# Two heads of the HGRN2 layer in one strand: the level products of both kept together on TensorE

## The chip, the cores and the metric

The kernel runs on one core of a Trainium2 chip. The metric is the device time of one launch in microseconds (us). The core's engines are TensorE (PE in the profile, PEld its weight loads), VectorE (DVE), ScalarE (ACT), GpSimd (POOL) and SyncE (SP); each works through its own queue in order, and they meet through semaphores.

## The reference

Two layers on x of shape 1 x 512 x 1024, float32. Layer 0 (mLSTM heads and sparse attention) is the same in both kernels. Layer 1 is cut here to what matters:

```python
h = rms_norm(x, norm_w[1])
fp, iv, qp, z = jnp.split(h @ w_in + b_in, 4, axis=-1)
logf = jnp.log(lb + (1.0 - lb) * jax.nn.sigmoid(fp))
k = (1.0 - lb) * jax.nn.sigmoid(-fp)
q = jax.nn.silu(qp)
# per head (8 heads of 128 channels):
#   S_t = diag(f_t) S_{t-1} + k_t v_t^T ;  o_t = S_t^T q_t
o = hgrn2_chunkwise(heads(q), heads(k), heads(iv), heads(logf))
o = rms_norm(o, head_norm)
x = x + (o * jax.nn.silu(z)) @ w_out
```

## The kernel before, in words

**Products.** A float32 product is made of three products of rounded operands: high by high, high by low, low by high. ACT writes the high half of a weight block (`whi`), VectorE the low half (`wlo`), 128 x 1024 at a time. One such product is a matmul of 128x512, the "large product" below; its results go to the banks `mx` and `my`.

**Layer 1.** The projection is cut into groups: `t0` to `t3` (forget and query columns of two heads each), `p0` and `p1` (a Strassen-like pair for the value and gate columns, whose extra operands are `ss`), then the output projection `o10`, `o11`. The list is in L2130 to L2140, in the order t0, p0, t1, t2, t3, p1, o10, o11. `t_evac` (L2071 to L2097) empties a `t` group: for each head it makes `f` and the tile `HB`, 128 x 3 x 512, which holds q, q times f, and k. `ivgg` is the tile of values and gates, filled by VectorE and multiplied on POOL.

**A head.** After the second head of a group, `t_evac` starts a strand `hgrn(h)` (L1888 to L2010) for each of the two. It computes the decayed scores of q and k by seven levels, l = 0 to 6, in which positions are joined into blocks of 2, 4, ... 128. Each level has small float32 products on TensorE, into a bank `sd` for levels 0 to 4 and `tq` for 5 and 6: 16 of 32x64 for level 0, 16 of 32x16 for levels 1 to 4, 8 of 32x32 for level 5, 4 of 64x64 for level 6. Then VectorE multiplies half of `HB` by products of the forget gates (`HB<-HB,f` at level 0, `HB<-HB,tt` after it), and the next level's products wait for that. After level 4 `copy_predicated` brings the scores into `AL`, and ACT copies them into the tile `f`. The state work follows: transposes (`tq<-cs,HB`), ACT's copy `kT`, products `tq<-ivgg,kT`, three VectorE steps into `Sx`, the output products `tq<-ivgg,f` and `tq<-Sx,HB`, squares on ACT, a root on POOL, four scaled copies `yo` on VectorE, four transposes `tq<-cs,yo`, and the copies `y1h` (ACT) and `y1l` (VectorE), which the output projection reads.

**What sets the order.** Nothing is issued as it is written. `Flow` (L452 to L516) runs the strands by rank; a strand yields what it waits for: marks, and free slots (`SDS` for an `sd` bank, `TQS` for a `tq` bank). `nlv` lets at most two heads be in their levels. The operations are recorded by `Plan` (L166 to L414), which schedules them over the engines with modelled costs, in several rounds, keeps the best, and then issues them all from one line, L410; so every instruction of the profile has that line, and tiles tell them apart. An operation recorded with `_join` must follow the one recorded before it on TensorE with nothing between: `Plan.edges` (L251 to L259) chains them and gives all their conditions to the first.

```python
        for a, b in zip(self.ops, self.ops[1:]):
            if a.eng == "T" == b.eng and (b.join or len(a.cols) < 4 and a.load == b.load and a.cols[0] < b.cols[0]):
                a.next = b
```

Layer 1 begins at about 340 us of the trace and runs to its end.

Of the kernel before, what the change touches and what calls it, by code (L numbers as in the profile page):

```python
# [15 lines left out]
I32 = mybir.dt.int32  # L16
AF = mybir.ActivationFunctionType
OP = mybir.AluOpType
# [10 lines left out]
HBN = 4  # L29
# [589 lines left out]
def build(tc, I, out):  # L619
# [6 lines left out]
    with ExitStack() as ctx:  # L626
# [24 lines left out]
        def sd_t():  # L651
            return pt("sd", 2)

        def tq_t():
            return pt("tq", 2)
# [324 lines left out]
        with ExitStack() as c0:  # L980
# [3 lines left out]
            def s_t(name, shape, bufs=2, dt=F32):  # L984
                return sp.tile(shape, dt, name=name, tag=name, bufs=bufs)
# [841 lines left out]
        with ExitStack() as c1:  # L1827
# [57 lines left out]
                    fl.mark(E1(n))  # L1885
                u_end(2)

            def hgrn(h):  # L1888
                yield [None, lambda: nlv[0] < 2, SDS]
                nlv[0] += 1  # L1890
                HB, f = HBs[h], fs[h]
                lv = sd_t()
                al, AT = AL[h % 2], cut(f, (4, 128))
                tot, toff, to = f, 0, 0
                tt = s_t("tt", [128, 512], 2)
                te = s_t("te", [128, 4], HBN)
                for l in range(7):
                    L = 1 << l
                    if l < 5:
                        for t in range(4):  # L1900
                            for b in range(4):
                                o = 128 * t + 32 * b
                                if l == 0:
                                    T.matmul(lv[32 * b:32 * b + 32, 64 * t:64 * t + 64], HB[:, 2, o:o + 32],
                                             cust(HB, [[512, 2], [1, 32]], o), start=True, stop=True,
                                             skip_group_check=True)
                                else:
                                    oo = 256 + 64 * (l - 1) + 16 * t
                                    T.matmul(lv[32 * b:32 * b + 32, oo:oo + 16], HB[:, 2, o:o + 32],
                                             cust(HB, [[2 * L, 16 // L], [1, L]], 512 + o + L), start=True,  # L1910
                                             stop=True, skip_group_check=True)
                    elif l == 5:
                        l2 = tq_t()
                        for t in range(8):
                            a, u, b = t // 4, t // 2 % 2, t % 2
                            o = 128 * (2 * a + b) + 64 * u
                            T.matmul(l2[64 * u + 32 * b:64 * u + 32 * b + 32, 32 * a:32 * a + 32], HB[:, 2, o:o + 32],
                                     HB[:, 1, o + 32:o + 64], start=True, stop=True, skip_group_check=True)
                    else:
                        l2 = tq_t()  # L1920
                        for t in range(4):
                            o, b = 128 * t, t % 2
                            T.matmul(l2[64 * b:64 * b + 64, 32 * (t - b):32 * (t - b) + 64], HB[:, 2, o:o + 64],
                                     HB[:, 1, o + 64:o + 128], start=True, stop=True, skip_group_check=True)
                    nb = 256 >> l
                    if L == 1:
                        w = cust(HB, [[512 - L, 2], [2, 256]], 512 + 1)
                        tr = cust(tot, [[1, 2], [2, 256]], toff)
                    else:
                        w = cust(HB, [[512 - L, 2], [2 * L, nb], [1, L]], 512 + L)  # L1930
                        tr = cust(tot, [[1, 2], [2, nb], [0, L]], toff)
                    V.tensor_tensor(w, w, tr, op=OP.mult)
                    m = fl.mark()
                    d_, to_ = (te, 0) if l == 6 else (tt, to)
                    V.tensor_tensor(d_[:, to_:to_ + nb], cust(tot, [[2, nb]], toff), cust(tot, [[2, nb]], toff + 1),
                                    op=OP.mult)
                    tot, toff, to = d_, to_, to + nb
                    if l == 0:
                        P.memset(f, 0.0)
                    if l == 5:  # L1940
                        for u in range(2):
                            for b in range(2):
                                A.activation(AT[64 * u:64 * u + 32, b::2, 64 * u + 32:64 * u + 64],
                                             cut(l2, (2, 32), slice(64 * u + 32 * b, 64 * u + 32 * b + 32)), AF.Copy)
                    if l == 6:
                        for b in range(2):
                            A.activation(AT[:64, b::2, 64:], cut(l2, (2, 64), slice(64 * b, 64 * b + 64)), AF.Copy)
                    if l == 4:
                        V.copy_predicated(al, cust(cs, [[0, 4], [1, 32]], SC["md"]).bitcast(I32),
                                          cut(lv[:, :256], (4, 64))[:, :, :32])  # L1950
                        V.copy_predicated(cust(al, [[32, 4], [2, 16]], 1), cust(mh0, [[0, 4], [1, 16]]).bitcast(I32),
                                          cust(lv, [[64, 4], [2, 16]], 33))
                        for l_ in range(1, 5):
                            L = 1 << l_
                            V.copy_predicated(cust(al, [[32, 4], [2 * L, 16 // L], [1, L]], L),
                                              cust(cs, [[0, 4], [L, 16 // L], [1, L]], SC["ml"] + 16 * (l_ - 1)).bitcast(I32),
                                              cust(lv, [[16, 4], [L, 16 // L], [1, L]], 256 + 64 * (l_ - 1)))
                        for b in range(4):
                            r_ = slice(32 * b, 32 * b + 32)
                            A.activation(AT[r_, :, r_], al[r_], AF.Copy)  # L1960
# [110 lines left out]
            def t_evac(pr):  # L2071
                def go(j4, p):
# [16 lines left out]
                    else:  # L2089
# [138 lines left out]
```

## Time and profile before

| | |
|---|---|
| time, median of 3 runs (range) | 612.31 us (611.69 to 613.61) |
| the profiled execution, its own time | 611.45 us |
| its span, first to last instruction | 609.7 us |
| TensorE busy | 601.4 us, 99% |
| VectorE busy | 472.8 us, 78% |
| ScalarE, GpSimd busy | 340.5 us, 56%; 123.7 us, 20% |
| moved by DMA | 102.84 MB, 169 GB/s on the mean |

The span is what the trace shows; the execution's own time holds what lies around it too. Busy times are those of the whole span. In the timelines a matmul's start is recorded, its end is modelled and overlaps the next start, so distances between starts are the thing to read on TensorE. The small float32 products are recorded twice each: a burst of 16 has x32 in the timeline, where the order has x16. Rows of one kind that follow each other are put together with their count.

### The profile page before, as it was taken

To read this page: it belongs to the slowest core of one execution; us is meant where nothing else is said; L and a number is where in the kernel's file an instruction comes from. 1 tells how busy PE (TensorE), PEld (TensorE's weight loads), DVE (VectorE), ACT (ScalarE), POOL (GpSimd) and SP (SyncE) were. 2 spreads that over 40 slices of the span, in tenths; PEclk is the share of its full clock that TensorE was granted. 3 is DMA by queue.
4 is the path that set the end of the run, shared out by engine and by line. 5 is a ranking of instruction groups with operands and counts; after the bars stand their busy time and mean duration, and the time that the engine had idled before them with its cause. 6 is when DMAs were issued, how large, how long until landed. Compare 5 with 4: busy or idle time off the path is not lost.

```text
span 609.7 us, 11829 instructions
## 1 busy us (share of the span) xinstructions
PE 601.4 (99%) x4458; PEld 484.0 (79%) x4458; DVE 472.8 (78%) x996; ACT 340.5 (56%) x886; POOL 123.7 (20%) x185
## 2 busy tenths in 40 slices
PE   9999999999999999999999999999999999999997
PEld 8888888877777767878888886778877877788886
DVE  5879998788898857789874588897788789987441
ACT  7466536666866655577544594455527275465400
POOL 1752461212022000014122401134010201022100
PEclk9999999999999999999999999999999999999999
DMA  9864079929339909564763952579553123573121
GB/s 322 266 247 145 11 240 267 285 70 299 102 63 279 206 9 250 183 227 120 275 202 122 328 173 73 173 231 230 144 126 104 37 69 110 188 284 114 34 77 62
DMA packets 29385, 102.84 MB, mean 169 GB/s; under 512 B 3856, under 2 KB 6800, under 8 KB 25488
## 3 DMA queue, kind: packets, MB, share of 16 engines
q1 hardware_dynamic: 24432, 72.43, 35.8%
q0 software_dynamic: 4608, 29.36, 19.3%
q8 instruction: 35, 0.57, 0.4%
q10 hardware_dynamic: 288, 0.30, 0.2%
q14 instruction: 22, 0.18, 0.1%
HBM read 95.79 MB, written 35.65 MB: 216 GB/s over the span
## 4 chain that ended last, share of the span: by engine, by line
PE 83%; DVE 8%; DMA 5%; issue 1%; ACT 1%; DVEq 0%; ACTq 0%
PE mm L410 29%; PE mx L410 16%; PE my L410 15%; PE sc L410 6%; PE ac L410 5%; PE tp L410 5%; PE tq L410 5%; DMA raw<-sxd 3%; DVE wlo L410 3%; PE sd L410 2%; DMA raw<-in_wall_dram 1%; DVE x L410 1%; DMA raw<-wt 1%; ACT whi L410 1%; DVE ivgg L410 1%
## 5 line engine op out<-in xcount | busy, mean ns | idle before, releaser
L410 ACT ACTIVATE whi<-raw 128x512 fp32r<-128x512 f32 (+1 forms) x196 | 111.6, 615 | 75.7 <-PE my L410 23.0
L410 DVE TENSOR_TENSOR wlo<-raw,whi 128x1024 fp32r<-128x1024 f32 (+1 forms) x102 | 121.2, 1195 | 26.7 <-ACT whi L410 24.2
L410 PE MATMUL mm<-whi,h0h 128*128 128x512 f32 (+1 forms) x148 | 59.4, 402 | 0.0
L410 PE MATMUL mm<-whi,h0l 128*128 128x512 f32 (+1 forms) x148 | 59.2, 400 | 0.0
L410 PE MATMUL mm<-wlo,h0h 128*128 128x512 f32 (+1 forms) x148 | 57.8, 396 | 0.0
L410 ACT ACTIVATE PP<-sc,nm 128x256 f32<-128x256 f32 (+3 forms) x56 | 30.7, 549 | 21.5 <-DVE nm L410 20.4
L410 DVE CUSTOM_DVE_ANT_0 sc<-sc,cz 128x384 f32<-128x384 f32 (+3 forms) x64 | 31.1, 504 | 13.2 <-PE sc L410 9.5
L410 PE MATMUL mm<-h0h,whi 128*128 128x512 f32 x96 | 38.9, 405 | 0.0
L410 PE MATMUL mm<-h0h,wlo 128*128 128x512 f32 x96 | 38.5, 401 | 0.0
L410 PE MATMUL mm<-h0l,whi 128*128 128x512 f32 x96 | 38.3, 399 | 0.0
L410 POOL TENSOR_SCALAR held<-wlo 128x1 f32<-128x1 f32 x32 | 10.7, 334 | 131.9 <-DVE wlo L410 119.8
L410 DVE TENSOR_TENSOR HB<-HB,tt 128x512 f32<-128x512 f32 x48 | 32.5, 699 | 3.9 <-PE sd L410 2.7
L410 PEld LDWEIGHTS mm<-wlo,h0h 128*128 128x128 f32 x148 | 27.9, 188 | 5.2 <-issue 0.2
L410 PEld LDWEIGHTS mm<-whi,h0l 128*128 128x128 f32 x148 | 27.9, 189 | 5.0 <-issue 0.2
L410 PEld LDWEIGHTS mm<-whi,h0h 128*128 128x128 f32 x148 | 28.0, 189 | 4.7
L410 POOL TENSOR_TENSOR ivgg<-ivgg,zz 128x256 f32<-128x256 f32 x16 | 16.2, 1025 | 64.9 <-ACT zz L410 64.7
L410 ACT ACTIVATE PT<-tp 128x384 f32<-128x384 f32 (+1 forms) x48 | 23.5, 526 | 7.4 <-PE tp L410 7.2
L410 PE MATMUL sc<-kd,q 128*128 128x256 f32 (+2 forms) x112 | 27.3, 338 | 0.0
L410 PE MATMUL my<-h1h,whi 128*128 128x512 f32 x64 | 26.0, 406 | 0.0
L410 PE MATMUL my<-h1l,whi 128*128 128x512 f32 x64 | 25.9, 405 | 0.0
L410 PE MATMUL mx<-h1l,whi 128*128 128x512 f32 x64 | 25.7, 402 | 0.0
L410 PE MATMUL mx<-h1h,wlo 128*128 128x512 f32 x64 | 25.7, 402 | 0.0
(387 smaller groups left out, 1616.0 us busy)
## 6 DMA issues: line engine op xcount, KB each, us to landing
raw<-in_wall_dram SPq DMA_DIRECT2D x74, 512.0 KB, 4.3
wt<-in_wall_dram POOLq DMA_DIRECT2D x18, 1024.0 KB, 11.7
raw<-wt SPq DMA_DIRECT2D x24, 512.0 KB, 3.7
wt<-wt POOLq DMA_DIRECT2D x6, 1024.0 KB, 11.2
sxd<-xsd POOLq DMA_DIRECT2D x6, 512.0 KB, 9.2
bias<-in_brow_dram SPq DMA_DIRECT2D x9, 256.0 KB, 7.9
xt<-in_xt_dram SPq DMA_DIRECT2D x8, 256.0 KB, 4.7
w<-in_cw_dram SPq DMA_DIRECT2D x2, 1024.0 KB, 9.6
```

The lines of the kernel that those rows point to most:

```text
L410: o.fn(*o.a, **k)
```

## The change

The body of `hgrn` is cut in three: `level_products`, `level_scale` and the rest, which keeps the name. A new strand `levels` takes one head or two through all seven levels: at each level first the products of every head, then their VectorE steps, then one wait for both. Within a head the products of a level are joined; for levels 1 to 4 the second head's products are joined to the first's. At its end the strand starts `hgrn` for each head. Heads 0 and 1, 2 and 3, 4 and 5 go in pairs; 6 and 7 get a strand each. The number and shapes of the instructions are the same on every engine. The diff, cut:

```diff
-            def hgrn(h):
-                yield [None, lambda: nlv[0] < 2, SDS]
-                nlv[0] += 1
...
-                for l in range(7):
...
-                    yield [m] + ([TQS] if 4 <= l < 6 else [])
-                nlv[0] -= 1
+            def level_products(x, l, join):
+
+                L, HB, lv = 1 << l, x.HB, x.lv
+                if l < 5:
+                    for t in range(4):
+                        for b in range(4):
+                            o = 128 * t + 32 * b
+                            k = dict(start=True, stop=True, skip_group_check=True, _join=join or t + b > 0)
...
+                x.l2 = l2 = tq_t()
+                if l == 5:
+                    for t in range(8):
...
+                                 HB[:, 1, o + 32:o + 64], start=True, stop=True, skip_group_check=True, _join=t > 0)
...
+            def level_scale(x, l):
...
+                V.tensor_tensor(w, w, tr, op=OP.mult)
+                x.m = fl.mark()
...
+            def levels(*heads):
+
+                xs = []
+                for h in heads:
+                    yield [None, SDS] + ([] if xs else [lambda: nlv[0] + len(heads) <= 2])
+                    nlv[0] += 1
+                    x = Mark()
+                    x.h, x.HB, x.f, x.al, x.lv = h, HBs[h], fs[h], AL[h % 2], sd_t()
...
+                    xs.append(x)
                 for l in range(7):
...
+                    for x in xs:
+                        level_products(x, l, x is not xs[0] and 0 < l < 5)
+                    for x in xs:
+                        level_scale(x, l)
+                    yield [x.m for x in xs] + ([TQS] if 4 <= l < 6 else [])
+                nlv[0] -= len(xs)
+                for x in xs:
+                    fl.add(hgrn(x), 1 + x.h)
+
+            def hgrn(x):
+                h, HB, AT, te, m = x.h, x.HB, x.AT, x.te, x.m
                 vs = slice(128 * (h % 2), 128 * (h % 2) + 128)
                 yield [m, TQS, E1("r%d" % (h // 2))]
...
-                        for a in (h - 1, h) if hh else ():
-                            fl.add(hgrn(a), 1 + a)
+                        for a in () if not hh else ((6,), (7,)) if h == 7 else ((h - 1, h),):
+                            fl.add(levels(*a), 1 + a[0])
```

The order of TensorE's queue for heads 0 and 1, levels 2 to 4, before. `HB_3649` is head 0, `HB_3665` head 1, and `sd_3685`, `sd_3688` their banks:

```order
L410 MATMUL my_3691<-wlo_3663,h1h_719 128x512
L410 MATMUL sd_3685<-HB_3649 32x16 x16
L410 MATMUL my_3691<-whi_3662,h1h_719 128x512
L410 MATMUL sd_3688<-HB_3665 32x16 x16
L410 MATMUL my_3691<-whi_3662,h1l_720 128x512
L410 MATMUL sd_3685<-HB_3649 32x16 x16
L410 MATMUL my_3691<-wlo_3663,h1h_719 128x512
L410 MATMUL sd_3688<-HB_3665 32x16 x16
L410 MATMUL my_3691<-whi_3669,h1h_719 128x512
L410 MATMUL sd_3685<-HB_3649 32x16 x16
L410 MATMUL my_3691<-whi_3669,h1l_720 128x512
L410 MATMUL sd_3688<-HB_3665 32x16 x16
```

The same heads with the change, levels 1 to 4, where "..." stands for large products:

```order
L410 MATMUL sd_3685<-HB_3649 32x16 x16
L410 MATMUL sd_3688<-HB_3665 32x16 x16
L410 MATMUL my_3699<-whi_3678,ss_3644 128x512
...
L410 MATMUL my_3700<-wlo_3682,ss_3644 128x512
L410 MATMUL sd_3685<-HB_3649 32x16 x16
L410 MATMUL sd_3688<-HB_3665 32x16 x16
L410 MATMUL my_3700<-whi_3681,ss_3644 128x512 x2
...
L410 MATMUL sd_3685<-HB_3649 32x16 x16
L410 MATMUL sd_3688<-HB_3665 32x16 x16
...
L410 MATMUL sd_3685<-HB_3649 32x16 x16
L410 MATMUL sd_3688<-HB_3665 32x16 x16
```

The lone bursts of 16, one large product apart, have become bursts of two times 16 with 9 to 20 large products between them.

The place where heads 2 and 3 end and heads 4 and 5 begin, with the change, on TensorE; `sd` rows are levels of heads 4 and 5, the `64x64` row is level 6 of heads 2 and 3, and the first "..." stands for five large products:

```order
L410 MATMUL tq<-HB 64x64 x8
L410 MATMUL sd<-HB 32x64 x32
L410 MATMUL tq<-cs,HB 128x128
L410 MATMUL my<-h1h,whi 128x512
...
L410 MATMUL tq<-cs,HB 128x128 x2
L410 MATMUL sd<-HB 32x16 x32
L410 MATMUL tq<-cs,HB 128x128 x3
L410 MATMUL my<-h1h,whi 128x512
L410 MATMUL tq<-ivgg,kT 128x128 x3
L410 MATMUL sd<-HB 32x16 x32
L410 MATMUL my<-h1l,whi 128x512
L410 MATMUL tq<-ivgg,f 128x128 x2
```

Before, the levels of heads 4 and 5 began partly after the outputs of head 2; now level 0 of both heads stands right behind level 6 of heads 2 and 3, and two more levels stand among their transposes and state products.

The end of the last head on TensorE, before. `tq<-cs,yo` are its transposes, and its `y1h` is first read by the product `mx_3974<-y1h_3984,whi_3961`:

```order
L410 MATMUL tq_4016<-cs_68,yo_4012 128x128 x2
L410 MATMUL mx_3965<-y1h_3984,whi_3961 128x512
L410 MATMUL tq_4016<-cs_68,yo_4012 128x128
L410 MATMUL mx_3965<-y1l_3985,whi_3961 128x512
L410 MATMUL mx_3965<-y1h_3984,wlo_3962 128x512
L410 MATMUL my_3968<-y1h_3984,whi_3961 128x512
L410 MATMUL my_3968<-y1l_3985,whi_3961 128x512
L410 MATMUL my_3968<-y1h_3984,wlo_3962 128x512
L410 MATMUL mx_3974<-y1h_3984,whi_3961 128x512
```

The same with the change, where `mx_3963<-y1h_3984,whi_3959` is that first reader:

```order
L410 MATMUL tq_4016<-cs_68,yo_4015 128x128 x2
L410 MATMUL mx_3969<-y1h_3984,wlo_3960 128x512
L410 MATMUL tq_4016<-cs_68,yo_4015 128x128
L410 MATMUL my_3970<-y1h_3984,whi_3959 128x512
L410 MATMUL tq_4016<-cs_68,yo_4015 128x128
L410 MATMUL my_3970<-y1l_3985,whi_3959 128x512
L410 MATMUL my_3970<-y1h_3984,wlo_3960 128x512
L410 MATMUL mx_3963<-y1h_3984,whi_3959 128x512
L410 MATMUL my_3968<-y1h_3984,whi_3959 128x512
```

Five large products stood between the last transpose and that reader, now two.

## Rows read from the trace of the kernel before

**Rows 1.** The page: busy time, share of the span and instructions of each engine.
```profile
PE 601.4 (99%) x4458; PEld 484.0 (79%) x4458; DVE 472.8 (78%) x996; ACT 340.5 (56%) x886; POOL 123.7 (20%) x185
```

**Rows 2.** Stretch 367 to 414: us, busy per engine (instructions), PE clock, DMA share, GB/s.
```profile
367.00:414.00 47.00, 46.35 (x540) 34.46 (x538) 43.17 (x67) 22.82 (x52) 8.71 (x10) 1.00 0.53 162
```

**Rows 3.** PE's timeline: start, duration, instruction, count; a joint burst of heads 2, 3.
```profile
450.14 0.39 PE L410 MATMUL my<-h1h,wlo 128*128 128x512 f32 x1
450.37 0.40 PE L410 MATMUL mx<-h1h,whi 128*128 128x512 f32 x1
450.70 0.74 PE L410 MATMUL sd<-HB 128*32 128x16 f32 x64
451.37 0.50 PE L410 MATMUL mx<-h1l,whi 128*128 128x512 f32 x1
451.71 0.39 PE L410 MATMUL mx<-h1h,wlo 128*128 128x512 f32 x1
451.93 0.40 PE L410 MATMUL my<-h1h,whi 128*128 128x512 f32 x1
452.26 0.33 PE L410 MATMUL tq<-HB 128*32 128x32 f32 x16
452.52 0.50 PE L410 MATMUL my<-h1l,whi 128*128 128x512 f32 x1
452.86 0.40 PE L410 MATMUL my<-h1h,wlo 128*128 128x512 f32 x1
```

**Rows 4.** PE's timeline, lone bursts of heads 0 and 1.
```profile
371.84 0.50 PE L410 MATMUL my<-whi,h1h 128*128 128x512 f32 x1
...
372.64 0.50 PE L410 MATMUL my<-whi,h1l 128*128 128x512 f32 x1
...
374.25 0.50 PE L410 MATMUL my<-whi,h1h 128*128 128x512 f32 x1
...
375.50 0.31 PE L410 MATMUL sd<-HB 128*32 128x16 f32 x14 [0.46 <-issue]
375.75 0.49 PE L410 MATMUL my<-whi,h1l 128*128 128x512 f32 x1
```

**Rows 5.** Waits of PE, 340 to 610: what waited, releaser, total, times, longest.
```profile
PE sd L410 <- issue: 0.5, 1, 0.5
PE sd L410 <- DVE HB L410: 0.4, 1, 0.4
PE tq L410 <- DVE Sx L410: 0.4, 1, 0.4
```

**Rows 6.** PE's timeline, a gap between large products.
```profile
378.04 0.40 PE L410 MATMUL mx<-whi,ss 128*128 128x512 f32 x1
378.50 0.70 PE L410 MATMUL my<-whi,ss 128*128 128x512 f32 x2
```

**Rows 7.** PE's weight loads, with idle time before them and its releaser.
```profile
411.45 1.42 PEld L410 LDWEIGHTS tq<-ivgg,kT 128*128 128x128 f32 x12 [0.45 <-ACT kT L410]
...
420.50 0.43 PEld L410 LDWEIGHTS tq<-cs,yo 128*128 128x128 f32 x4 [0.47 <-DVE yo L410]
```

**Rows 8.** VectorE's timeline, heads 0 and 1.
```profile
375.87 0.69 DVE L410 TENSOR_TENSOR HB<-HB,tt 128x512 f32<-128x512 f32 x1 [0.78 <-PE sd L410]
...
377.61 0.74 DVE L410 SCALAR_TENSOR_TENSOR ivgg<-my,rs,ivgg 128x512 f32<-128x512 f32 x1
...
415.32 2.19 DVE L410 TENSOR_TENSOR wlo<-raw,whi 128x1024 fp32r<-128x1024 f32 x1
```

**Rows 9.** VectorE's instructions by form, 340 to 610: count, busy us, mean ns, idle before.
```profile
L410 DVE TENSOR_TENSOR wlo<-raw,whi 128x1024 fp32r<-128x1024 f32 x48 | 61.2, 1282 | 6.7 <-ACT whi L410 6.6
```

**Rows 10.** POOL's timeline beside the last of rows 8.
```profile
414.71 1.71 POOL L410 TENSOR_TENSOR ivgg<-ivgg,zz 128x256 f32<-128x256 f32 x2
```

**Rows 11.** All engines' timeline: last yo transpose and the copy after it.
```profile
577.87 0.27 PE L410 MATMUL tq<-cs,yo 128*128 128x128 f32 x1
...
578.33 0.67 ACT L410 ACTIVATE y1h<-tq,pcs 128x512 fp32r<-128x512 f32 x1
```

More of the change, by code (lines that the diff above doesn't have):

```diff
@@ new lines, in level_products @@
+            def level_products(x, l, join):
[5 more added lines that the diff above has]
+                            k = dict(start=True, stop=True, skip_group_check=True, _join=join or t + b > 0)
+                            if l == 0:
+                                T.matmul(lv[32 * b:32 * b + 32, 64 * t:64 * t + 64], HB[:, 2, o:o + 32],
+                                         cust(HB, [[512, 2], [1, 32]], o), **k)
+                            else:
+                                oo = 256 + 64 * (l - 1) + 16 * t
+                                T.matmul(lv[32 * b:32 * b + 32, oo:oo + 16], HB[:, 2, o:o + 32],
+                                         cust(HB, [[2 * L, 16 // L], [1, L]], 512 + o + L), **k)
+                    return
+                x.l2 = l2 = tq_t()
+                if l == 5:
+                    for t in range(8):
+                        a, u, b = t // 4, t // 2 % 2, t % 2
+                        o = 128 * (2 * a + b) + 64 * u
+                        T.matmul(l2[64 * u + 32 * b:64 * u + 32 * b + 32, 32 * a:32 * a + 32], HB[:, 2, o:o + 32],
+                                 HB[:, 1, o + 32:o + 64], start=True, stop=True, skip_group_check=True, _join=t > 0)
+                else:
+                    for t in range(4):
+                        o, b = 128 * t, t % 2
+                        T.matmul(l2[64 * b:64 * b + 64, 32 * (t - b):32 * (t - b) + 64], HB[:, 2, o:o + 64],
+                                 HB[:, 1, o + 64:o + 128], start=True, stop=True, skip_group_check=True, _join=t > 0)
@@ new lines, in level_scale @@
+            def level_scale(x, l):
+                L, HB, f, lv, al, AT, tot, toff, to = 1 << l, x.HB, x.f, x.lv, x.al, x.AT, x.tot, x.toff, x.to
+                nb = 256 >> l
+                if L == 1:
+                    w = cust(HB, [[512 - L, 2], [2, 256]], 512 + 1)
+                    tr = cust(tot, [[1, 2], [2, 256]], toff)
+                else:
+                    w = cust(HB, [[512 - L, 2], [2 * L, nb], [1, L]], 512 + L)
+                    tr = cust(tot, [[1, 2], [2, nb], [0, L]], toff)
+                V.tensor_tensor(w, w, tr, op=OP.mult)
+                x.m = fl.mark()
+                d_, to_ = (x.te, 0) if l == 6 else (x.tt, to)
+                V.tensor_tensor(d_[:, to_:to_ + nb], cust(tot, [[2, nb]], toff), cust(tot, [[2, nb]], toff + 1), op=OP.mult)
+                x.tot, x.toff, x.to = d_, to_, to + nb
+                if l == 0:
+                    P.memset(f, 0.0)
+                if l == 5:
+                    for u in range(2):
+                        for b in range(2):
+                            A.activation(AT[64 * u:64 * u + 32, b::2, 64 * u + 32:64 * u + 64],
+                                         cut(x.l2, (2, 32), slice(64 * u + 32 * b, 64 * u + 32 * b + 32)), AF.Copy)
+                if l == 6:
+                    for b in range(2):
+                        A.activation(AT[:64, b::2, 64:], cut(x.l2, (2, 64), slice(64 * b, 64 * b + 64)), AF.Copy)
+                if l == 4:
+                    V.copy_predicated(al, cust(cs, [[0, 4], [1, 32]], SC["md"]).bitcast(I32),
+                                      cut(lv[:, :256], (4, 64))[:, :, :32])
+                    V.copy_predicated(cust(al, [[32, 4], [2, 16]], 1), cust(mh0, [[0, 4], [1, 16]]).bitcast(I32),
+                                      cust(lv, [[64, 4], [2, 16]], 33))
+                    for l_ in range(1, 5):
+                        L = 1 << l_
+                        V.copy_predicated(cust(al, [[32, 4], [2 * L, 16 // L], [1, L]], L),
+                                          cust(cs, [[0, 4], [L, 16 // L], [1, L]], SC["ml"] + 16 * (l_ - 1)).bitcast(I32),
+                                          cust(lv, [[16, 4], [L, 16 // L], [1, L]], 256 + 64 * (l_ - 1)))
+                    for b in range(4):
+                        r_ = slice(32 * b, 32 * b + 32)
+                        A.activation(AT[r_, :, r_], al[r_], AF.Copy)
```

71 lines of the change are left out of this document (2 added, 69 removed).

## The prediction

> **What bounds the kernel now.** I read the engines' shares first: TensorE (PE) is busy for 601.4 of 609.7 us, 99%, VectorE (DVE) for 472.8 [rows 1]. So the time can only fall if TensorE's own stream gets shorter or stops less. The granted clock is 1.00 in every stretch used here [rows 2]. The stream is mostly 128x512 products, which start 0.23 us apart, with bursts of small products between them; what a burst costs is the distance between the starts of the large products around it, less the 0.23 us that they need anyway, plus what the second large one loses. In 367 to 414 us, where heads 0 and 1 go through their levels, VectorE works 43.17 of 47.00 us [rows 2], so it is close behind TensorE there; the reader should see that a change which helps TensorE by a few us meets VectorE next. The waits that the waits view names on TensorE in layer 1 are few: 0.5 and 0.4 us before level products, 0.4 us before the output products [rows 5].
>
> **The price of a burst.** With both heads together, 32 products of 32x16: large products start at 450.14, 450.37, 451.37 and 451.71 [rows 3]. The first gap is 1.00, the next 0.34, against 0.23 each: 0.77 + 0.11 = 0.88 us. With one head alone, 16 products between single large ones, the starts at 371.84 and 372.64 are 0.80 apart: 0.57 us [rows 4]. Two lone bursts cost 1.14, the joint one 0.88, so joining saves 0.26. From another pair of shapes: twice 16 more products cost 0.88 - 0.57 = 0.31, so one small product is about 0.019; eight of 32x32 at 452.26 cost 0.36 + 0.11 = 0.47 [rows 3], which less 8 x 0.019 leaves 0.32 as the fixed part. I take 0.29 for each burst that vanishes, between 0.26 and 0.32. Here the Trainium skill gives a smaller price. "TensorEngine Tiling (Array Packing)", Key Properties, says that changing the tiling mode drains TensorE, and "TensorE: Matmul & The Clock Gate" gives a drain of about 128 cycles; as an estimate from these pages, two changes a burst at 2.4 GHz would be 0.11 us. By that the ten bursts below would give 1.1 us and not 2.9; the rows do not agree, and they decide.
>
> **What the change removes.** No instruction goes and none is added on any engine; layer 0 keeps its order. The orders have 38 bursts with level products before, 28 now. Heads 0 and 1 account for five: 12 before (one for level 0, one for level 1, six lone ones for levels 2 to 4, four for levels 5 and 6), 7 now. Ten bursts by 0.29 are **-2.9 us** (-2.6 to -3.2). A further -0.3 at most may come from fewer switches between 64-row and 32-row shapes inside one burst; that stays in the range.
>
> **Waits that go.** (a) At 374.25 to 375.75 a lone level burst of heads 0 and 1 stops in its middle, for 0.46 at 375.50: 1.50 apart where 0.23 + 0.57 would do, 0.70 us [rows 4]. The strand's levels there are one large product apart. In the new order 9 to 30 large products (2.1 us or more) stand between levels of heads 0 and 1, more than the two HB products of VectorE (0.69 us each [rows 8]) need. Gone: 0.70. (b) Two gaps inside the large products that follow, 378.04 to 378.50, 0.23 too much [rows 6], and one of the same size four us later. The later product needs the bank my, which VectorE's ivgg step at 377.61 empties only by 378.35 [rows 8], being queued behind an HB product and a weight split; I take 0.48 as gone. (c) The kT products of heads 0 and 1 wait for ACT's kT copy, 0.45 us [rows 7], which stands behind copies that wait for VectorE. Now 17 more large products (3.9 us) come before them. Gone: 0.45. Together **-1.6 us** (0 to -1.7).
> What stays: the 0.4 us for Sx (again five large products between kT and the output products), the 0.47 us before the yo transposes [rows 7] (again 11), and heads 6 and 7, which remain two strands with a few large products per level (0.4 us [rows 5]).
>
> **Waits that come.** (d) The tail. The last yo transposes used to be followed by five large products before y1h of the last head was needed, now by two. After the last transpose at 577.87 the ACT copy starts at 578.33 and takes 0.67 [rows 11], 1.13 us in all; two large products cover some 0.57. So 0.5 us (0 to 1.1, if ACT is in a weight copy). (e) The crowded place where heads 2 and 3 end while heads 4 and 5 begin: two level bursts, both kT groups and the outputs stand one large product apart. VectorE's HB pairs, Sx and yo must keep up. Before, the yo transposes waited 0.47 with 11 large products ahead of them [rows 7]; here nine and a burst stand ahead. I take 0.2 more, between 0 and 0.5, nearer nothing because of the extra burst. Together **+0.7 us** (0 to 1.6). SP, POOL and the weight transfers have no instruction moved past a level by more than the large products carry it; I cost them at nothing: ACT works 22.82 and POOL 8.71 of the 47 us [rows 2].
>
> **Sum.** -2.9 - 1.6 + 0.7 = -3.8. The profiled execution took 611.45, so it would take 607.65; it lies 0.86 under the median of 612.31, so the forecast for a median is 612.31 - 3.8 = **608.5 us**. About 0.3%, 1.84 us, can be told from no change.
>
> **Does VectorE keep up?** For heads 0 and 1 TensorE's stretch becomes 47.0 + 3.9 (17 more large products) - 1.45 (five bursts) - 1.63 (waits) = 47.8 us before the state work. VectorE has one weight split (wlo, 1.28 [rows 9]) and one ivgg step (0.74 [rows 8]) more to do there: 43.2 + 2.0 = 45.2. That leaves 2.6 us in which it may stand idle.
>
> **Rivals.**
> *Bound by VectorE* (B). It used its idle 3.8 us of this stretch because of waits like that at 375.87, 0.78 us for TensorE's products [rows 8]. If it can't do with 2.6, TensorE's savings for heads 0 and 1 (1.45 + 1.63) come back as waits for wlo or HB: -3.8 + 3.1 = -0.7, 611.6 us. For it: 43.17 of 47.00. Against: the joint levels are spread, so the queue has other work.
> *Slower* (C). One level step of both heads puts two HB products in a row on VectorE, both behind one burst, and the queue is in order: if every step of heads 0 and 1 and of heads 4 and 5 leaves VectorE idle 0.78 us as at 375.87, it loses 12 x 0.78 = 9.4 us and has 2.6 to spare: +6.8 on TensorE, 615.3 us. It decides from where a step costs heads 0 and 1 more than 2.6 / 6 = 0.43 us and the crowded place anything. POOL would worsen it: a wlo at 415.32 took 2.19 us [rows 8] beside two POOL multiplies that lasted 1.71 together [rows 10], against a mean of 1.28 [rows 9]. The Trainium skill ("SBUF — State Buffer", shared port pair) says that VectorE and GpSimd hold this port exclusively and the loser blocks; the row agrees. A large product that stands behind a waiting burst waits too: after the 0.46 us stop at 375.50 the next large one starts only at 375.75 [rows 4]. Against C: between levels there is other VectorE work in the new order.
> *Joining saves nothing* (D): each head's part brings its own fixed cost, or the nine pairs that stood together already were all that could. Then only waits change: -1.6 + 0.7, 611.4 us; by the drain price above, 610.3. Against: 1.14 against 0.88.
> *All waits go* (E): also 0.4 for Sx, 0.4 for heads 6 and 7, 0.47 for yo, nothing new, 0.32 a burst: -3.2 - 1.6 - 1.3 = -6.1, 606.2 us.
>
> **How the numbers follow.** Forecast 0.61 (its own range 607.0 to 610.2), E 0.11, B 0.16, C 0.06, D 0.06. Faster by over 0.3% (under 610.47) are the forecast, E, and a little of D and B: 0.76. Within 0.3%: the rest of B and D, 0.18. Slower: C, 0.06. The range reaches from below E, 605.3 (with the shape switches and a low run), to B, 611.6.
>
> **What would show it.** In the new profile: 15 bursts of 32 products of 32x16 at 0.85 to 0.92 us each; joint 32x32 and 64x64 bursts about 0.29 under two lone ones; no stop inside a level burst of heads 0 to 5; a wait of about 0.5 us on y1h in the tail; VectorE busy about 45 of 48 us where heads 0 and 1 go through their levels. I am wrong if large products wait for wlo or HB there (B, C), or if the joint burst costs over 1.05 us (D).

## The result, and the profile after

The changed kernel takes 607.66 us (median of 6 runs, 606.25 to 607.87) against 611.66 for the kernel before (median of 6 runs, 610.03 to 613.61): 4.0 us less, ratio 0.9929 (0.9910 to 0.9949). The forecast was -3.8 us, from a median of 612.31.

The page of the changed kernel: TensorE is still busy for 99% of the span, and the span is 3.9 us shorter, all of it in TensorE's busy time (601.4 before [rows 1]); VectorE is busy for 77% (78% before).

```profile
span 605.8 us, 11820 instructions
...
PE 597.3 (99%) x4458; PEld 484.6 (80%) x4458; DVE 469.4 (77%) x996; ACT 340.8 (56%) x886; POOL 125.5 (21%) x185
```

The gain is all in layer 1. In TensorE's timeline I take as its length the time from the first root product (`tq<-cs,rs`) to the start of TensorE's last product. Before, these start at 348.71 and 605.59: 256.88 us. In the changed kernel:

```profile
350.35 0.27 PE L410 MATMUL tq<-cs,rs 128*128 128x128 f32 x1
...
601.93 0.28 PE L410 MATMUL mx<-y1h,wlo 128*128 128x256 f32 x1
```

251.58 us, 5.3 less. What lies ahead of layer 1 has the same instructions in the same order, yet its end differs from one execution to the next: the root product starts between 348.40 and 352.13 us over the 13 profiles of this study, with kernels that do not differ there, and 1.5 us of that is visible at once in this profile, whose first products of layer 0 stand 0.24 us apart until 9.8 us, where those of the kernel before stand 0.13 apart from 7 us on; the granted clock reads 1.00 in both, so it doesn't tell the two apart. Times therefore scatter by some us, and the experiments are read by the length of layer 1 first.

Bursts in TensorE's timeline of the changed kernel, of two shapes (start, duration, instruction, count):

```profile
374.25 0.40 PE L410 MATMUL my<-whi,ss 128*128 128x512 f32 x1
374.58 0.74 PE L410 MATMUL sd<-HB 128*32 128x16 f32 x64
375.25 0.50 PE L410 MATMUL my<-whi,ss 128*128 128x512 f32 x1
375.58 0.39 PE L410 MATMUL my<-wlo,ss 128*128 128x512 f32 x1
...
392.62 0.40 PE L410 MATMUL mx<-wlo,ss 128*128 128x512 f32 x1
392.95 0.46 PE L410 MATMUL tq<-HB 128*32 128x32 f32 x32
393.34 0.73 PE L410 MATMUL mx<-whi,ss 128*128 128x512 f32 x2
393.90 0.39 PE L410 MATMUL mx<-wlo,ss 128*128 128x512 f32 x1
```

The joint burst of 32x16 puts the large products 1.00 and 0.33 us apart: 0.87 us, as the joint ones of the kernel before [rows 3]. The joint 32x32 burst at 392.95 puts them 0.72 apart, and the row after the x2 row starts at 393.90, 0.56 later: 0.72 + 0.56 for three intervals, 1.28 - 0.69 = 0.59, where two lone ones of 0.47 were 0.94. A joint 64x64 one at 400.52, read in the same way, costs 0.94 + 0.57 - 0.69 = 0.82, where two lone ones of 0.575 were 1.15 (before, the large products around the one at 384.57 start 0.70 and 0.34 apart).

VectorE in the stretch of heads 0 and 1 (370 to 418, as wide as [rows 2] and one us more) is busy 45.35 of 48 us, about the 45.2 of 47.8 that the prediction worked out:

```profile
370.00:418.00 48.00, 47.44 (x562) 37.59 (x561) 45.35 (x76) 23.97 (x56) 12.03 (x15) 1.00 0.66 182
```

The waits that the waits view names on TensorE in layer 1 (total, times, longest) are others than before [rows 5]; the stop named issue and the wait for Sx are gone:

```profile
PE tq L410 <- ACT kT L410: 0.6, 1, 0.6
PE my L410 <- DVE tt L410: 0.4, 1, 0.4
PE sd L410 <- DVE HB L410: 0.4, 1, 0.4
PE mx L410 <- ACT y1h L410: 0.3, 1, 0.3
```

The kT wait, first in ACT's timeline of the kernel before. There the two kT copies stand ahead of six of the eight score copies (`f<-AL`):

```profile
410.26 0.63 ACT L410 ACTIVATE f<-AL 32x128 f32<-32x128 f32 x2 [1.30 <-DVE AL L410]
410.91 0.87 ACT L410 ACTIVATE kT<-tq 128x384 f32<-128x384 f32 x2
411.81 1.92 ACT L410 ACTIVATE f<-AL 32x128 f32<-32x128 f32 x6
```

With the change, in the timeline of all engines, the score copies of both heads stand ahead of kT. VectorE's last copy into `AL` ends at 412.40 (412.34 before); the second head's four score copies wait for it and hold kT's copy to 413.73:

```profile
411.91 0.49 DVE L410 COPY_PREDICATED AL<-cs,sd 128x64 f32<-128x64 int32 x2
...
412.44 1.27 ACT L410 ACTIVATE f<-AL 32x128 f32<-32x128 f32 x4 [0.24 <-DVE AL L410]
...
413.73 0.87 ACT L410 ACTIVATE kT<-tq 128x384 f32<-128x384 f32 x2
...
414.27 1.49 PE L410 MATMUL tq<-ivgg,kT 128*128 128x128 f32 x11 [0.56 <-ACT kT L410]
```

Heads 6 and 7, where two strands remain:

```profile
513.49 1.84 DVE L410 TENSOR_TENSOR HB<-HB,tt 128x512 f32<-128x512 f32 x2 [0.27 <-PE sd L410]
...
513.92 0.86 POOL L410 TENSOR_TENSOR ivgg<-ivgg,zz 128x256 f32<-128x256 f32 x1 [1.34 <-ACT zz L410]
...
514.52 0.45 PE L410 MATMUL sd<-HB 128*32 128x16 f32 x32
...
515.38 0.44 PE L410 MATMUL sd<-HB 128*32 128x16 f32 x32 [0.41 <-DVE HB L410]
```

The two HB products take 1.84 us beside POOL's multiply, and the level burst stops in its middle for 0.41. The tail:

```profile
575.76 0.27 PE L410 MATMUL tq<-cs,yo 128*128 128x128 f32 x1
...
576.07 0.69 ACT L410 ACTIVATE y1h<-tq,pcs 128x512 fp32r<-128x512 f32 x1 [1.81 <-PE tq L410]
576.10 0.40 PE L410 MATMUL my<-y1h,wlo 128*128 128x512 f32 x1
...
576.81 0.50 PE L410 MATMUL mx<-y1h,whi 128*128 128x512 f32 x1 [0.31 <-ACT y1h L410]
```

The last transpose starts at 575.76, the copy ends at 576.76, and the first reader of y1h comes 0.71 us after the large product ahead of it in place of 0.23: 0.48 us of new wait.

### The profile page after: what moved, and what is told of

It is laid out like the page before. It is cut to its first block, busy times and chain, and to the rows that moved or that the text cites. A ratio compares the mean times of both kernels' runs of the same rounds, so it can differ in the third digit from the quotient of the medians.

```text
span 605.8 us, 11820 instructions
## 1 busy us (share of the span) xinstructions
PE 597.3 (99%) x4458; PEld 484.6 (80%) x4458; DVE 469.4 (77%) x996; ACT 340.8 (56%) x886; POOL 125.5 (21%) x185
## 4 chain that ended last, share of the span: by engine, by line
PE 87%; DVE 6%; DMA 4%; ACT 2%; issue 1%; DVEq 0%; ACTq 0%
PE mm L410 29%; PE mx L410 18%; PE my L410 15%; PE sc L410 6%; PE ac L410 6%; PE tp L410 5%; PE tq L410 5%; DMA raw<-sxd 3%; PE sd L410 2%; DVE wlo L410 1%; DVE x L410 1%; DVE HB L410 1%; DVE q L410 1%; DMA raw<-in_wall_dram 1%; ACT h0h L410 1%
## 5 line engine op out<-in xcount | busy, mean ns | idle before, releaser
L410 DVE TENSOR_TENSOR wlo<-raw,whi 128x1024 fp32r<-128x1024 f32 (+1 forms) x102 | 119.7, 1180 | 28.5 <-ACT whi L410 26.4
L410 POOL TENSOR_TENSOR ivgg<-ivgg,zz 128x256 f32<-128x256 f32 x16 | 17.5, 1104 | 75.3 <-ACT zz L410 75.3
L410 PE MATMUL mx<-h1h,whi 128*128 128x512 f32 x64 | 25.6, 400 | 0.0
```

Source lines behind the costliest of these rows:

```text
L410: o.fn(*o.a, **k)
```

## The experiments

Lengths are those of layer 1 as defined above, in us. The figures 261.0 and 255.5 in two of the expectations run to the end of the span, which lies some 4 us later; 252.3 and 257.5 include the last product's 0.28.

| run | length of layer 1 | median time (runs) |
|---|---|---|
| before, two profiles | 256.88, 256.61 | 611.66 (6), 611.54 (1) |
| changed kernel, two profiles | 251.58, 252.49 | 607.66 (6), 609.09 (7) |
| only heads 0 and 1 in one strand | 254.29 | 608.43 (12) |
| no chain between the heads | 251.91 | 606.94 (6) |
| bursts taken apart | 258.47 | 613.78 (10) |
| no multiply on POOL | 251.09 | 606.91 (4) |
| kT copy first | 255.74 | 611.98 (10) |
| heads 6 and 7 paired | 251.38 | 606.62 (4) |
| levels doubled | 281.97 | 638.29 (1) |
| four pairs, no chain | 251.26 | 606.30 (9) |
| four pairs, yo chained | 251.41 | 607.69 (5) |

The runs were made in sets, and the kernel before was timed in each. Its medians were 611.66 beside the result; 611.60 beside the two kernels again, heads 0 and 1, and the kernel without the chain; 612.13 beside the next four rows of the table; 610.89 beside the doubled levels and the four pairs; 610.90 beside the last. The ratios below are to these.

On the mean the change takes 4.7 us off layer 1 (256.75 to 252.04).

**The two kernels again.** The edit is none.

> The kernel before, profiled a second time. If the stop of 0.46 us inside a level burst of heads 0 and 1 (named issue) comes from the order, it stands again at the same burst. If it is the instruction supply of one execution, it is elsewhere or missing. From the first root product of layer 1 to the end of the span the first profile has 261.0 us; I expect 260.0 to 261.5. At the start of layer 0 the products were 0.13 us apart from 6.2 us on before, and 0.24 apart until 9.8 us with the change: if that is luck of a run, this profile can have either.

256.61 us, within 0.3. The stop at 375 us is 0.28 us where it was 0.70 (the large products around that burst start at 374.55 and 375.63), and another one stands where the first profile has only 0.2 us, in a level 5 burst of heads 2 and 3:

```profile
454.11 0.27 PE L410 MATMUL tq<-HB 128*32 128x32 f32 x8
454.94 0.27 PE L410 MATMUL tq<-HB 128*32 128x32 f32 x8 [0.56 <-issue]
```

So their length does not belong to the order: one place, at 375 us, stops in both executions of this program, another in one of them. Here layer 0 ran at the short distance from 5.9 us on.

> The changed kernel again, profiled and timed. Main theory (ten bursts fewer at 0.29 us, waits gone and come): 4 to 5.5 us under before; layer 1 from its first root product to the end 255.5 us, as in the first profile. Rival (the 1.5 us that the slow start cost in the first profile belong to the changed kernel): the slow start again, and a time of 607.7. If the slow start is luck of a run, this profile or some of the runs show 606.2 instead.

609.09 us against 611.60, 2.5 us less, ratio 0.9951 (0.9927 to 0.9974), runs from 605.95 to 611.13: the scatter is wider than the question, and the gain of this set is smaller than the first one's 4.0. The wide distance at the start belongs to that execution and not to the kernel: here the products stand 0.13 apart from 5.8 us on, and 1.3 us against the first profile are lost elsewhere in layer 0 (246 to 266 us). All waits of layer 1 stand again at the same places within 0.01 us, but for one that the first profile doesn't have: 0.5 us on VectorE's ivgg at 535 us. It also stands in three of the runs below, with 0.2 to 1.1 us, and accounts for most of the difference of 0.9 us between the two lengths.

**Only heads 0 and 1 in one strand.**

```diff
-                        for a in () if not hh else ((6,), (7,)) if h == 7 else ((h - 1, h),):
+                        for a in () if not hh else ((h - 1, h),) if h == 1 else ((h - 1,), (h,)):
```

> Only heads 0 and 1 go in one strand; heads 2 to 7 get a strand each. TensorE's order has 33 bursts with level products, against 38 before and 28 with the change. Burst theory: five bursts at 0.29 us are 1.5, and the stop (0.70) and the two bank gaps (0.48) of heads 0 and 1 go: 2.7 us under before, 1.5 to 3.3, so about 609.0. Rival (VectorE takes back what heads 0 and 1 save): under 0.8 us. Rival (the whole gain is in heads 0 and 1): 4 us.

Ratio 0.9954 (0.9936 to 0.9971), 608.43 us, which the times of the same set do not part from the whole change (609.09); layer 1 is 2.46 us under before, in the middle of what the burst theory gave. And it had a new stop, the longest of all with these bursts, at a level burst of heads 2 and 3:

```profile
PE sd L410 <- issue: 1.4, 1, 1.4
```

Without it the run would have been near 253, some 3.8 us under before and close to the 4 us of the other rival; with the stops of the kernel before (0.5 and 0.6 us named) left out as well, some 3.3. So that the length lies in the middle of the range is partly luck, and how the gain divides between heads 0 and 1 and the rest is not settled by this run. VectorE took nothing back. With every head in a strand of its own, the new code gives TensorE the very order of the kernel before, so the two-head strand is what acts, not the joining within a head.

**No chain between the heads' products.**

```diff
-                        level_products(x, l, x is not xs[0] and 0 < l < 5)
+                        level_products(x, l, False)
```

> The strands of two heads stay, but the second head's products are no longer chained to the first's; the planner may part them. Its order has 26 bursts with level products, two fewer than with the change. Burst theory: as the changed kernel, 0.6 us less, within 0.5 of it for what the order moves. Rival (the chain to the first head is what gives the gain, by keeping both heads' products from being parted): 2 us or more slower than the changed kernel.

Layer 1 251.91, 0.1 less than the changed kernel's mean; the time 606.94, ratio 0.9923 (0.9904 to 0.9943). The chain is not needed: with both heads' products recorded one after the other and due at the same time, the planner puts them together itself.

**Bursts taken apart.** A flag on the second head's first product of a level; when the plan is issued, the next large product is put ahead of it:

```diff
+        for o in [o for o in todo if o.apart]:
+            i = todo.index(o)
...
+            d = next(p for p in todo[i:] if p.eng == "T" and p.a[0].tensor.name[:3] in ("mx_", "my_"))
+            if not any(q in todo[i:] for q in d.pred):
+                todo.remove(d)
+                todo.insert(i, d)
```

> The changed kernel, with one large product moved in between the two heads' products of 20 level steps of heads 0 to 5. The order of every other engine is that of the changed kernel; TensorE has 70 bursts in layer 1 where it has 52, all of them with the same products. Main theory (a burst costs 0.29 us beside its body): 18 x 0.29 = 5.2 us more in layer 1, 4.7 to 5.8. By the drain price of the skill's pages (0.11 us) 2.0 us. Rival (the gain came from the waits and the spreading, and a burst's cost is hidden): under 1 us. Two profiles of the changed kernel have 252.3 us on the mean from the first root product of layer 1 to TensorE's last product; here about 257.5.

Layer 1 is 258.47, 6.4 us over the changed kernel; 613.78 us, ratio 1.0035 (1.0013 to 1.0057): slower than the kernel before. One of the 20 places in TensorE's timeline (it answers to 374.25 to 375.58 above):

```profile
374.37 0.40 PE L421 MATMUL my<-whi,ss 128*128 128x512 f32 x1
374.69 0.45 PE L421 MATMUL sd<-HB 128*32 128x16 f32 x32
375.07 0.50 PE L421 MATMUL my<-whi,ss 128*128 128x512 f32 x1
375.50 0.45 PE L421 MATMUL sd<-HB 128*32 128x16 f32 x32
375.88 0.50 PE L421 MATMUL my<-wlo,ss 128*128 128x512 f32 x1
376.21 0.63 PE L421 MATMUL my<-whi,ss 128*128 128x512 f32 x2
```

374.37 to 376.21 is 1.84 us for three intervals of large products: 1.84 - 0.69 = 1.15, against 0.87 with the pair kept together (the pairs of levels 0, 5 and 6, read in the same way, differ by 0.33 to 0.34). The split costs 0.28 us, and 20 of them 5.6 (counted by the large products between them there are 18 more bursts, since two of the halves came to stand beside another burst); the other 0.8 are waits: the burst stretches hold 0.25 more of them than the changed kernel's, and the ivgg wait near 540 us is 0.6 in this execution. Nothing hid a burst's fixed part here. The Trainium skill's drain ("TensorE: Matmul & The Clock Gate"), as an estimate 0.11 us for the two changes of mode of a burst, would have made the 20 places 2.2 us; the measurement decides, and it says 0.28 each or a little more.

**No multiply on POOL.**

```diff
-                    P.tensor_tensor(gi, gi, zz, op=OP.mult)
+                    P.memset(zz, 0.0, _price=687.6)
```

> Leaves out the gate multiply on POOL (gate times z); in its place POOL fills the scratch tile, and the planner is told the same cost. The order on TensorE is that of the changed kernel. Theory (POOL's reads stretch VectorE's splits and HB products, and that ends two of the waits left): the mean weight split falls to 1.22 us, the pair of HB products of heads 6 and 7 that took 1.84 takes 1.3, the stop of 0.4 us on HB there goes, the kT wait of heads 0 and 1 falls from 0.9 to about 0.5: 0.6 to 1.3 us less in layer 1. Rival (the stretch is hidden everywhere): under 0.3 us.

Layer 1 251.09, 0.95 less than the changed kernel's mean, which is inside the theory's range, and 0.5 less than its faster profile, which is just outside; 606.91 us. VectorE's rows by form (count, busy us, mean ns) of the changed kernel:

```profile
L410 DVE TENSOR_TENSOR wlo<-raw,whi 128x1024 fp32r<-128x1024 f32 x48 | 60.1, 1256 | 8.9 <-ACT whi L410 8.4
L410 DVE TENSOR_TENSOR HB<-HB,tt 128x512 f32<-128x512 f32 x48 | 32.4, 706 | 3.2 <-PE tq L410 1.6 <-PE sd L410 0.9 <-DVE tt L410 0.5
```

and the same two without POOL's multiply:

```profile
L410 DVE TENSOR_TENSOR wlo<-raw,whi 128x1024 fp32r<-128x1024 f32 x48 | 58.3, 1220 | 10.2 <-ACT whi L410 9.8
L410 DVE TENSOR_TENSOR HB<-HB,tt 128x512 f32<-128x512 f32 x48 | 31.5, 687 | 3.8 <-PE tq L410 1.6 <-PE sd L410 1.5 <-DVE tt L410 0.5
```

The stretch is gone, and it did end waits: TensorE's kT wait is no longer named (the large products around its burst start 1.83 us apart, where they were 2.32; the same twelve products without a wait, at 546 us of the changed kernel, take 1.49: 0.34 us late in place of 0.83), and the level burst that answers to 514.52 above runs through. In TensorE's timeline the next one then stops instead:

```profile
514.88 0.32 PE L410 MATMUL sd<-HB 128*32 128x16 f32 x16
...
515.55 0.59 PE L410 MATMUL sd<-HB 128*32 128x16 f32 x48 [0.36 <-issue]
```

so part of the gain is given back to a stop named issue. The Trainium skill ("SBUF — State Buffer", shared port pair) names the cause of the stretch, two SBUF inputs on VectorE beside a GpSimd instruction that reads SBUF; here all of the stretch goes with POOL's reads, while its fill stays.

**ACT's kT copy ahead of the score copies.** In this edit the score copies of heads 2 to 5 read an `AL` that the next pair may already have overwritten, so their scores are other data; the instructions and their sizes are the same.

```diff
-                    for b in range(4):
-                        r_ = slice(32 * b, 32 * b + 32)
-                        A.activation(AT[r_, :, r_], al[r_], AF.Copy)
...
                 A.activation(flat(kT), kp[:, :384], AF.Copy)
+                for b in range(4):
+                    r_ = slice(32 * b, 32 * b + 32)
+                    A.activation(AT[r_, :, r_], x.al[r_], AF.Copy)
```

> The changed kernel with ACT's four score copies (f from AL) recorded behind its kT copy and not ahead of it. Theory (kT stands behind copies that wait for VectorE): the kT wait of heads 0 and 1, 0.9 us, goes. The new order has 56 bursts, four more than the change, of 128-wide products, at about 0.1 to 0.2 us each: 0.3 us less in layer 1, from 0.9 less to 0.5 more. Rival (kT waits for VectorE anyway, or the output products wait for the score copies in its place): no gain or a loss.

The rival: the kT wait is gone, and layer 1 is 3.7 us longer than the changed kernel's. The planner, given another list, moved the whole order, and other waits took the place: the waits view of TensorE names 1.2 us for yo, 1.1 for ivgg and 0.8 for y1h. It says nothing on the kT copy alone, since everything else moved with it.

**Heads 6 and 7 paired.**

```diff
-                        for a in () if not hh else ((6,), (7,)) if h == 7 else ((h - 1, h),):
+                        for a in () if not hh else ((h - 1, h),):
```

> Heads 6 and 7 in one strand as well: 27 bursts with level products, one fewer than the change (0.3 us). Theory (VectorE is the bound where heads 6 and 7 go through their levels, a few large products apart): the waits there, 1.3 us with the change, stay within 0.5, so 0.3 us less in layer 1, between 0.8 less and 0.5 more. Rival (the two separate strands make the waits): 1 us less or more than that.

The rival was right on the place: with one strand the waits of heads 6 and 7, 1.3 us in the changed kernel, are gone. VectorE has the same work to do there, so it was not its amount that made TensorE wait but the close spacing of two interleaved strands: the joint bursts of levels 1 to 4 now start 3 to 4 us apart. But a wait of 1.5 us stands at the end, so the length stays inside the theory's range:

```profile
PE mx L410 <- ACT y1h L410: 1.5, 1, 1.5
```

ACT makes the squares of head 7 before y1h of head 6. Layer 1 is 251.38, 0.66 under the changed kernel; 606.62 us, ratio 0.9905 (0.9876 to 0.9934), which does not part it from the changed kernel.

**Levels doubled.**

```diff
+                                for r in range(2):
-                                T.matmul(lv[32 * b:32 * b + 32, oo:oo + 16], HB[:, 2, o:o + 32],
+                                    T.matmul(lv[32 * b:32 * b + 32, oo:oo + 16], HB[:, 2, o:o + 32],
```

> Every product of levels 1 to 4 is issued twice in a row, inside the same bursts (the second writes the same values): 512 more products of 32x16 and as many weight loads. Main theory (a burst has a fixed part of 0.29 us, one more product 0.0185): 512 x 0.0185 = 9.5 us more in layer 1, less what the planner hides in waits, 8.5 to 10.5; no more than the fixed part for the bursts themselves. Rival on the stops named issue (the instruction supply of TensorE limits long series of small products): the doubled bursts of 64 products stop inside, waits named issue add up to over 2 us, and layer 1 is over 12 us longer. If a product's own price were 0.57 / 16 = 0.036 us (no fixed part), 18 us more.

29.9 us more in layer 1. Two neighbouring bursts of the same kind, one without a stop and one with:

```profile
379.64 0.39 PE L410 MATMUL my<-whi,ss 128*128 128x512 f32 x1
379.96 1.43 PE L410 MATMUL sd<-HB 128*32 128x16 f32 x128
381.32 0.50 PE L410 MATMUL my<-whi,ss 128*128 128x512 f32 x1
381.66 0.40 PE L410 MATMUL my<-wlo,ss 128*128 128x512 f32 x1
...
383.58 0.73 PE L410 MATMUL sd<-HB 128*32 128x16 f32 x54
385.46 0.93 PE L410 MATMUL sd<-HB 128*32 128x16 f32 x74 [1.15 <-issue]
```

Without a stop, 64 products of 32x16 cost 1.68 + 0.34 - 0.46 = 1.56 us where 32 cost 0.87: 0.0215 for one more product, so 512 are 11 us. The rest is stops and what they bring:

```profile
PE sd L410 <- issue: 7.2, 6, 1.9
PE tq L410 <- issue: 3.5, 2, 1.9
```

10.7 us of stops named issue, in 8 places of up to 1.9 us, always inside or just behind a long series of small products and never among large ones. Named waits for VectorE (HB and yo) are 4.2 us more. The order moved too: it has 24 bursts with level products, four fewer than the change, and from 529 to 542 us level products follow each other with no large product between them, with three stops. The granted clock falls there: 0.83 of the higher level on the mean of 520 to 550 (the third column from the end), and 0.50 to 0.52, the lower level, from 536 to 546:

```profile
520.00:550.00 30.00, 23.62 (x644) 18.60 (x643) 21.97 (x45) 10.90 (x28) 2.87 (x4) 0.83 0.28 82
```

so the large products from 542.66 to 545.64 are 0.43 us apart in place of 0.23. After the stop of 1.9 us at 469.78 it is 0.91 in 460 to 480. The rival on the supply of instructions gave over 2 us of such stops and over 12 more in all, and is the one that holds. Which queue brings TensorE's instructions can be read from the pages: 512 more products and weight loads, and nothing else, raise the blocks of 16 KB that q8 moves from 35 in the changed kernel to 43 (packets, MB, share of the DMA engines' time).

```profile
q8 instruction: 35, 0.57, 0.4%
...
q8 instruction: 43, 0.70, 0.4%
```

The packets' times in the traces tie the stops to it. Each of the 8 stops ends 1.3 to 1.6 us after a block of q8 has landed: the one above ends at 385.46, and a block was under way from 383.15 to 384.03. It is the same for the five stops told of in the profiles with normal levels, the one of 0.28 us among them (1.2 to 1.5 us; in the first profile of the kernel before, a block from 373.09 to 374.02 and the end of the stop at 375.50). Many blocks land without a stop, as in the changed kernel, where one arrives from 373.29 on and no stop is named.

**Four pairs without a chain, and with the yo transposes chained.** Both edits above for the first; for the second also

```diff
-                    T.transpose(tp[:, 128 * t:128 * (t + 1)], yo[:, t, :], idf)
+                    T.transpose(tp[:, 128 * t:128 * (t + 1)], yo[:, t, :], idf, _join=t > 0)
```

> Four strands of two heads, and no chain between the two heads' products: 49 bursts in layer 1 (52 with the change), 26 with level products. Burst theory: two or three bursts less, 0.6 to 0.9 us; the waits of heads 6 and 7 (1.3 us) gone as in the run with heads 6 and 7 paired: 1 to 2 us less in layer 1 than the changed kernel, if no wait on y1h or kT grows in their place. Rival (the planner moves the wait to the end, as there): the same as the changed kernel within 0.7.

251.26, 0.78 under the changed kernel's mean: the rival's figure, or just over it. 606.30 us, ratio 0.9929 (0.9911 to 0.9947), the same ratio as the changed kernel's first. The wait for y1h at the end is again 1.5 us.

> As the run with four unchained pairs, and the four yo transposes of a head are chained. There the transposes of head 6 were parted by the output products of head 7, and ACT made the squares of head 7 before y1h of head 6, so TensorE waited 1.5 us for y1h. In this order the four stand together ahead of those products, and twelve large products follow before y1h is read. Theory: that wait goes; after the last head's four transposes the first reader of y1h comes at once, so a wait of 0.9 to 1.2 us there takes the place of it: 0.3 to 0.9 us less in layer 1 than with four unchained pairs (251.3 from the first root product to the start of TensorE's last product). Rival: ACT keeps its order, the wait only moves: no gain.

251.41: no gain, the rival again. 607.69 us, ratio 0.9932 (0.9908 to 0.9957). The wait for y1h fell to 0.8, and one of 0.4 for yo stands ahead of it.

No version beats the changed kernel by more than the runs can tell: by layer 1 the four pairs lie 0.2 to 0.3 us under its faster profile, and its own two profiles are 0.9 us apart.

## Why the prediction was right, and where it was not

The sign, the size and the range held: -4.0 us by the times of the result, -2.5 by those of the second set, -4.7 by layer 1 on the mean of two profiles each, against -3.8. Its steps did not all hold.

- **Ten bursts fewer, -2.9 us.** Right in kind and a little small. Ten at the measured savings, 0.27 for 32x16 (1.14 less 0.87), 0.35 for 32x32 and 0.33 for 64x64, are 3.0, and the fewer shape switches that the prediction left in the range add some 0.3 (estimate from the burst costs of both traces, whose sum without waits falls by 3.5 us). The run with the bursts taken apart is the test: 0.28 us a split, nothing hidden.
- **(a) The stop of 0.70 us goes.** Right in size for the first profile (it was 0.28 in the second), wrong in its reason. The step said that the strand's levels, one large product apart, waited for VectorE. The second profile of the kernel before, the doubled levels and the landing times of q8 show a stop of TensorE's own instruction stream, which comes where many small products follow closely and not always in the same burst. Neither profile of the changed kernel has one in these bursts; whether the wider spacing of the levels took it away or chance did is not shown, since two nearby kernels have one elsewhere.
- **(b) The two gaps of 0.48.** Right: no gap of that kind is left in the stretch of heads 0 and 1.
- **(c) The kT wait goes, -0.45.** Wrong. It grew: the weight loads now stand idle 0.99 us before kT (0.45 in [rows 7]), and by the starts of the large products the burst is 0.83 us late where it was 0.28. The step took it that kT stands behind the same copies as before and gains the time of the large products. TensorE did come later, but the order of ACT's queue changed: before, the two kT copies went ahead of six of the eight score copies, the second head's four among them; with one strand for both heads all eight score copies go ahead of kT, and the last waits for VectorE's `AL` copy, which ends at 412.40, as late as before (412.34). The 2.6 us in which VectorE may stand idle were there (48 - 45.35), but not ahead of that copy: beside a POOL multiply one of its HB products of that strand, at 404.89, took 1.12 us in place of 0.69, and without POOL's reads the burst was 0.49 less late.
- **What stays.** The wait for Sx (0.4 named, 0.60 by the large products around that burst, 3.87 us apart before and 3.27 now) was to stay and went, and so did the 0.47 before the yo transposes (0.25 by the same reading, and 0.2 before the next four): TensorE came to both later, since it had already waited for kT. Together that undoes what (c) missed, 1.0 us. Heads 6 and 7 were to keep their 0.4; they wait 1.3.
- **(d) The tail, +0.5.** Measured 0.48.
- **(e) The crowded place, +0.2.** Measured about nothing: its bursts stand at what the same products cost elsewhere in the trace, within 0.15 us each (estimate).

So the ten bursts are the part of the sum that the runs bear out; that the waits came out near the forecast too is luck, since the misses of 0.5 to 1 us in (c), in what stays and in heads 6 and 7 have both signs. Rival B (VectorE gives back what heads 0 and 1 save) fell with the run of those heads alone, 2.5 us of gain. Rival C showed in two places, at kT and at heads 6 and 7, where POOL stretches VectorE, worth some 1 us and not 6.8. Rival D fell by the 0.28 us a split, and rival E, in which every wait goes, by the waits at kT, at heads 6 and 7 and in the tail.

## What to carry to other kernels

A burst of small products between large ones costs a fixed part, here 0.28 us, that nothing hid on a full TensorE: count the bursts of the order before and after, and price them by the distance of the large products around them. This holds for the products of 32 and 64 rows or columns alone: groups of 128x128 products show no fixed part in the changed kernel (four transposes at 556.8 cost 0.45 us, six at 542.1 0.67, twelve kT products at 546.0 1.35, so 0.11 each); no run here split those. Two independent chains that both need such bursts are worth keeping in step for that reason alone, and the planner here kept them together once they were recorded together and due together. A wait between two engines close to each other does not vanish by giving one more work ahead of it: ask which queue holds the producer, what the change puts ahead of it there, and what stretches that engine.

## What the runs showed that was not expected

TensorE stops, with nothing to wait for, inside long series of small products: 0.28 to 1.4 us in single places of the profiles with normal levels, and with the series doubled 8 places of up to 1.9 us, 10.7 in all. The stops change in length, and some in place, between executions of the same program. All 13 end 1.2 to 1.6 us after the queue that brings TensorE's instructions has landed a block, so as far as the traces can show TensorE waits there for its instructions; no run changed their supply alone. Why a block comes too late at one place and not at another no run here shows. Why layer 0, which is the same in all these kernels, ends up to 3.7 us apart stays open as well.
